# A zero-write on POOL between the additions of a depthwise convolution

## The chip, the core and the metric

The kernel runs on one core of one Trainium2 chip. The metric is the device time of one execution in microseconds. TensorE (PE) multiplies, VectorE (DVE), ScalarE (ACT) and GpSimd (POOL) do the elementwise work, SyncE (SP) and POOL issue DMAs.

## The reference

The computation is a two-layer decoder trunk over 512 tokens of width 1024, in float32. Layer 0 is a Conformer convolution module and a SwiGLU feed-forward; layer 1 is grouped-query attention in a sliding window over a shared K/V, and a second feed-forward. What matters here is the convolution module:

```python
a = glu(x @ w_pw1 + b_pw1)                      # first pointwise projection
y = causal_depthwise_conv(a, w_dw) + b_dw       # 31 taps, each channel by itself
y = silu(layernorm(y, ln_g, ln_b))
h = h + y @ w_pw2 + b_pw2                       # second pointwise projection
h = h + swiglu_ffn(rmsnorm(h), w_up, w_down)
```

## The kernel before

Channels lie on the partitions in eight tiles of 128; the 512 tokens are worked in two halves of 256 columns. The depthwise convolution of one half (class `Half`) goes through the channel tiles in pairs. Of the 31 taps of a tile some go to DVE, which multiplies and adds in one instruction into a PSUM bank (L1009). The others go to ACT and POOL: ACT makes the product of a tap in one of eight buffers `pr` (L1001), POOL adds it to the running sum (L1002). In the second half 17, 15, 15 and 15 taps of a tile go this way, for the four pairs. At the end of a tile POOL adds the two sums (L1013), ACT squares the result (L1038), and TensorE sums over the channels with a matrix of ones (L1052, L1058).

The first half's convolution runs beside the first projection. The second half's runs on, as a background job, beside the first half's second projection (`pw2`, L378, then L1143 for the residual) and the first part of its feed-forward (`ffn_part`, `ffn_up`); `pace` advances it by due points, one call per weight chunk. Before that job starts, 20 of its steps are taken beside the last first projections (`N_EARLY`) and 7 between the rows of the first half. A step of a pair advances both of its tiles by one DVE tap and by the products and additions that belong to it.

From the feed-forward on each weight chunk of 128x1024 is split into a rounded part `whi` (ACT, L294) and a remainder `wlo` (DVE, L297), and each product is three matmuls (L380 to L382): 24 for a chunk. The splits run up to three chunks ahead in four buffers. The norm before the feed-forward is taken late: TensorE sums the squares (L503), DVE finishes the mean (L505), POOL raises it to the power -1/2 (L507), ACT puts it on a diagonal (L515), TensorE spreads it over the partitions (L529), and the evacuation of the first pair of banks uses it.

The second half's feed-forward part 0 (`twin=True`) scales its result with the same spread norm on POOL (L606), and DVE adds it to the residual (L607).

Beside its arithmetic POOL issues DMAs that add weight blocks in DRAM (`prepare`, L289). Each is ordered behind the last instruction that went through the helper `pool_op`, which only notes that instruction. The helper `tc.issue_after(ins)` puts an instruction behind another on the same engine without a semaphore. The order of each engine's queue is otherwise made at compile time, from a schedule.

Of the kernel before, what the change touches and what calls it, by code (L numbers as in the profile page):

```python
# [11 lines left out]
F32 = mybir.dt.float32  # L12
# [6 lines left out]
P = 128  # L19
# [190 lines left out]
def hybrid_trunk(ctx: ExitStack, tc: tile.TileContext, xT, W, prm_in, wdw_in, sinks, relb, onehot, fin, lead, out):  # L210
    nc = tc.nc
    cpool = ctx.enter_context(tc.tile_pool(name="const", bufs=1))
# [9 lines left out]
    def uid(s):  # L222
        ctr[0] += 1
        return f"{s}{ctr[0]}"

    def bank():
        return ps.tile([P, 512], F32, tag="bank", name=uid("bank"))
# [4 lines left out]
    def temp():  # L232
        return tmp.tile([P, 512], F32, tag="tmp", name=uid("tmp"))
# [23 lines left out]
    def load(upto):  # L257
        while stream["dma"] < min(len(PLAN), upto):
# [3 lines left out]
            raws[i] = r  # L262
            stream["dma"] += 1

    def pool_op(op):
        pooled[0] = op.ins
        return op

    def copy_sums(name, lo, hi):
# [57 lines left out]
    def job(gen, *points):  # L327

        jobs.append([gen, points, 0])
# [32 lines left out]
    def get(*key):  # L362
        advance()
        pace()
        due[0] += rate[0]
        tick(int(due[0]))
        due[0] -= int(due[0])
        i = stream["use"]
        assert PLAN[i] == key, (PLAN[i], key)
        stream["use"] += 1  # L370
        hi, lo = splits.pop(i)
        n = {"kv": 4, "up": 4, "q": 4}.get(key[0], 2)
        sh = dict(a=n)
        return tuple(w and w.rearrange("p (a b) -> p a b", **sh) for w in (hi, lo))
# [32 lines left out]
    def mm2(out, w, x, start, stop):  # L407

        first, second = (w[0], x, out), (w[1], x[:, 0, :], out[:, 0, :])
        if stop:  # L410
            first, second = second, first
        nc.tensor.matmul(first[2], first[0], first[1], start=start, stop=False)  # L412
        nc.tensor.matmul(second[2], second[0], second[1], start=False, stop=stop)  # L413
# [59 lines left out]
    def col(name, i):  # L473
        c = PARAM_COLS[name] + i
        return prm[:, c:c + 1]
# [75 lines left out]
    def accs(w):  # L551
        if w == 512:
            return [bank() for _ in range(4)]
        return [b[:, e * w:(e + 1) * w] for b in (bank(), bank()) for e in range(2)]
# [8 lines left out]
    def down_group(keys, act_of, banks, on_step=None, on_m=None):  # L563
        nk = len(keys)
        w = banks[0].shape[-1]
        for ci, (key, kts) in enumerate(keys):
            whi, wlo = get(*key)
            order = [(k, m) for k in range(2) for m in range(4)]
            if ci == nk - 1:
                order = [(k, m) for m in range(4) for k in range(2)]  # L570
            for k, m in order:
                sl = slice(m * P, (m + 1) * P)
                mm3(banks[m], (whi[:, k, sl], wlo and wlo[:, k, sl]), act_of(kts + k),
                    ci == 0 and k == 0 and opens(m, w), ci == nk - 1 and k == 1 and closes(m, w))
                if on_step is not None and ci < nk - 1 and m == 3:
                    on_step()
                if on_m is not None and ci == nk - 1 and k == 1:
                    on_m(m)
                    if m % 2:
                        on_step()  # L580
            if on_step is not None and on_m is None and ci == nk - 1:
                on_step()
                on_step()

    def ffn_part(layer, part, xg, tok, rms, on_h=None, twin=False, plain=None):
        lo, hi = HALVES0[part]
        hid = ffn_up(layer, lo, hi, xg, tok, rms, twin, plain)
        w = tok.stop - tok.start
        for g in range(2):
            if twin:  # L590
                banks = [bank().rearrange("p (a s) -> p a s", a=2) for _ in range(4)]
                for kp in range(lo, hi):
                    whi, wlo = get("down", layer, kp, g)
                    order = [(k, m) for k in range(2) for m in range(4)]
                    if kp == hi - 1:
                        order = [(k, m) for m in range(4) for k in range(2)]
                    for k, m in order:
                        sl = slice(m * P, (m + 1) * P)
                        mm2(banks[m], (whi[:, k, sl], wlo[:, k, sl]), hid.both(2 * (kp - lo) + k),
                            kp == lo and k == 0, kp == hi - 1 and k == 1)  # L600
                rs_bc = rms.step2()
                for m, b in enumerate(banks):
                    t, hm = temp()[:, 0:w], h[g * 4 + m][:, tok]
                    nc.scalar.copy(t, b[:, 1, :])
                    nc.vector.tensor_add(t, b[:, 0, :], t)
                    pool_op(nc.gpsimd.tensor_mul(t, t, rs_bc))  # L606
                    nc.vector.tensor_add(hm, hm, t)  # L607
                continue
            if w == 256:

                full = [bank().rearrange("p (a s) -> p a s", a=2) for _ in range(2)]
                banks = [b[:, e, :] for b in full for e in range(2)]
            else:
                banks = accs(w)
            down_group([(("down", layer, kp, g), 2 * (kp - lo)) for kp in range(lo, hi)],
                       lambda kt: hid[kt], banks)
            if w == 256:
                rs_bc = rms.step2().unsqueeze(1).to_broadcast([P, 2, w])
                for e, b in enumerate(full):
                    i = g * 4 + 2 * e  # L620
                    nc.vector.tensor_mul(b, b, rs_bc)
                    nc.vector.tensor_add(hT[:, i:i + 2, tok], b, hT[:, i:i + 2, tok])
                    for k in range(2 if on_h is not None else 0):
                        on_h(i + k)
                continue
            for m in range(4):
                t = h[g * 4 + m][:, tok]
                nc.vector.tensor_add(t, banks[m], t)
                if on_h is not None:
                    on_h(g * 4 + m)  # L630
# [303 lines left out]
    with tc.tile_pool(name="conv", bufs=2) as cv:  # L934
# [41 lines left out]
        class Half:  # L976
# [7 lines left out]
            def taps(self, ct, c):  # L984
                n_pool = N_POOL[self.hf][ct // 2]
                a = a_pad[ct][:, self.hf * W2:(self.hf + 1) * W2 + PAD]
                yt = self.y[:, ct, :]

                def tap(j):
                    return wdw[:, ct, j:j + 1]  # L990

                nd = TAPS - n_pool
                acc, pi = None, 0
                for i in range(nd):
                    while pi * nd < n_pool * (i + 1):
                        j = nd + pi
                        pr = cv.tile([P, W2], F32, tag="pr", name=uid("pr"), bufs=8)
                        if acc is None:
                            on_act = nc.scalar.activation(pr, a[:, j:j + W2], AF.Identity, scale=tap(j), bias=col("bdw", ct))
                        else:  # L1000
                            on_act = nc.scalar.mul(pr, a[:, j:j + W2], tap(j))  # L1001
                            on_pool = pool_op(nc.gpsimd.tensor_add(pr, acc, pr))  # L1002
                        acc = pr
                        pi += 1
                    src = a[:, i:i + W2]
                    if i == 0 and ct < 4:
                        nc.vector.tensor_scalar(c, src, tap(i), None, op0=ALU.mult)
                    else:
                        on_dve = nc.vector.scalar_tensor_tensor(yt if i == nd - 1 else c, src, tap(i),  # L1009
                                                                c if i else self.shift, op0=ALU.mult, op1=ALU.add)  # L1010
                    yield
                self.last = on_act.ins, on_dve.ins, on_pool.ins
                pool_op(nc.gpsimd.tensor_add(yt, yt, acc))  # L1013
# [186 lines left out]
        for at_, (hf, ct) in enumerate(projs):  # L1200
# [13 lines left out]
            while done < n_taps * min(1, (at_ + 1) / 11):  # L1214
                next(taps, None)
                done += 1
# [23 lines left out]
            late.gate()  # L1240
        h1.after = [h0.silu]
        base = seen[0]
        job(second, (base, 0), (base + 8, 19), (base + 13, 22), (base + 26, 40), (base + 30, 45), (base + 34, 50), (base + 35, h1.n_steps - early - 3))
        x0 = {"ffn0": Pairs(KT)}
        plain = quads.tile([P, KT, W2], F32, tag="quad", name=uid("plain"))
# [70 lines left out]
    job(rows0.sums(), (base + 11, 0), (base + 19, 8), (base + 26, 14), (base + 32, 17))  # L1316
    pw2(h1.z, n1)
    ffn_part(0, 0, x0["ffn0"], HALF[1], n1.rms, twin=True)
    flush()

# [30 lines left out]
    if True:  # L1351
# [24 lines left out]
        for half in range(2):  # L1376
# [7 lines left out]
            if half == 0:  # L1384
                rs_bc = rms.step2()
# [312 lines left out]
```

## Time and profile before

| | us |
|---|---|
| median of 3 runs (1043.19 to 1044.5) | 1043.42 |
| the profiled execution | 1043.27 |
| its span, first to last instruction | 1041.5 |
| TensorE busy in the span | 1031.5 |
| POOL busy in the span | 473.2 |
| POOL's additions L1002, 208 of them | 155.4 |

A line of a timeline reads: start in microseconds from the start of the span, length, engine, line of the kernel, operation, tiles written and read, shapes, count of merged instructions, and in brackets the idle time of the engine before it with what ended that. A line of a group has busy time, mean duration in ns of one, and idle time before. A line of waits has the waiting instruction, what it waited for, the total in microseconds, how often, and the longest.

### The profile page before, as it was taken

How to read it: one execution, taken by the hardware profiler on the slowest of the kernel's cores; microseconds unless marked ns; L12 is line 12 of the kernel's file. 1: busy time of each engine (PE TensorE's matmuls, PEld its weight loads, DVE VectorE, ACT ScalarE, POOL GpSimd, SP SyncE). 2: the span in 40 equal slices, each digit the busy share in tenths (PEclk: the TensorE clock that was granted, in tenths of full speed). 3: DMA queues.
4: the chain of work that ended last, by engine and by line, in shares of the span. 5: the costliest groups of instructions: out<-in, count | busy, mean ns of one | idle time of the engine just before them, and what ended most of it. 6: DMA issues, size and time to landing. Idle time of an engine off the chain costs nothing.

```text
span 1041.5 us, 17709 instructions
## 1 busy us (share of the span) xinstructions
PE 1031.5 (99%) x6580; PEld 932.6 (90%) x6580; DVE 776.5 (75%) x1202; ACT 613.0 (59%) x1062; POOL 473.2 (45%) x569
## 2 busy tenths in 40 slices
PE   9999999999999999999999999999999999999996
PEld 8888889999988999998888877788989999898995
DVE  3999989978789777673536566678686877868777
ACT  3887798847776556552333565466655556554654
POOL 3999999930535233221214255405442334434134
PEclk9999999999999999999999999999999999999998
DMA  9999747999999988999969766955879988877742
GB/s 356 340 315 207 205 126 204 272 256 275 249 239 262 304 220 284 256 301 244 286 209 254 210 183 183 228 154 152 252 230 312 287 264 264 245 233 222 224 150 81
DMA packets 67282, 248.33 MB, mean 238 GB/s; under 512 B 7579, under 2 KB 13884, under 8 KB 66364
## 3 DMA queue, kind: packets, MB, share of 16 engines
q1 hardware_dynamic: 54236, 200.75, 55.9%
q0 software_dynamic: 12672, 46.14, 24.8%
q8 instruction: 51, 0.84, 0.3%
q10 hardware_dynamic: 288, 0.31, 0.1%
q14 instruction: 35, 0.29, 0.1%
HBM read 241.93 MB, written 97.52 MB: 326 GB/s over the span
## 4 chain that ended last, share of the span: by engine, by line
PE 98%; DMA 0%; DVE 0%; issue 0%; POOLq 0%; SPq 0%; POOL 0%; ACT 0%
PE bank L380 20%; PE bank L382 20%; PE bank L381 20%; PE bank L960 10%; PE bank L902 9%; PE bank L412 4%; PE bank L378 4%; PE bank L413 2%; PE bank L1441 1%; PE bank L1483 1%; PE bank L1470 1%; PE bank L1058 1%; PE bank L1607 1%; PE bank L948 1%; DMA both<-in_lead_dram 0%; PE bank L1562 0%
## 5 line engine op out<-in xcount | busy, mean ns | idle before, releaser
L297 DVE TENSOR_TENSOR wlo<-raw,whi 128x1024 fp32r<-128x1024 f32 x246 | 329.7, 1348 | 136.8 <-ACT whi L294 136.5
L294 ACT CAST whi<-raw 128x1024 fp32r<-128x1024 f32 x246 | 257.1, 1049 | 276.6 <-PE bank L381 194.1
L380 PE MATMUL bank<-quad,whi 128*128 128x256 f32 (+1 forms) x976 | 307.4, 317 | 0.0
L381 PE MATMUL bank<-quad,whi 128*128 128x256 f32 (+1 forms) x976 | 306.6, 315 | 0.0
L382 PE MATMUL bank<-quad,wlo 128*128 128x256 f32 (+1 forms) x976 | 305.7, 315 | 0.0
L380 PEld LDWEIGHTS bank<-quad,whi 128*128 128x128 f32 x976 | 185.5, 191 | 12.8 <-issue 1.6
L381 PEld LDWEIGHTS bank<-quad,whi 128*128 128x128 f32 x976 | 186.0, 191 | 11.9 <-issue 0.5
L382 PEld LDWEIGHTS bank<-quad,wlo 128*128 128x128 f32 x976 | 185.6, 191 | 11.8 <-issue 0.4
L853 POOL TENSOR_TENSOR up<-up 128x512 f32<-128x512 f32 x34 | 62.9, 1851 | 283.6 <-ACT up L850 283.6
L1002 POOL TENSOR_TENSOR pr<-pr,pr 128x256 f32<-128x256 f32 x208 | 155.4, 788 | 2.6 <-ACT pr L1001 2.5
L380 PE MATMUL bank<-rows,whi 128*128 128x256 f32 x488 | 138.0, 283 | 0.0
L381 PE MATMUL bank<-rows,whi 128*128 128x256 f32 x488 | 137.8, 282 | 0.0
L382 PE MATMUL bank<-rows,wlo 128*128 128x256 f32 x488 | 137.8, 282 | 0.0
L1009 DVE SCALAR_TENSOR_TENSOR bank<-apad,wdw,bank 128x256 f32<-128x256 f32 x248 | 112.4, 485 | 3.4
L1001 ACT ACTIVATE pr<-apad,wdw 128x256 f32<-128x256 f32 x208 | 98.3, 502 | 14.9 <-POOL pr L1002 13.1
L960 PE MATMUL bank<-quad,w 128*128 128x256 f32 x448 | 98.7, 380 | 0.0
L960 PEld LDWEIGHTS bank<-quad,w 128*128 128x128 f32 x448 | 84.9, 190 | 11.8 <-DVE bank L1009 0.2
L380 PEld LDWEIGHTS bank<-rows,whi 128*128 128x128 f32 x488 | 93.1, 191 | 0.3
L381 PEld LDWEIGHTS bank<-rows,whi 128*128 128x128 f32 x488 | 93.1, 191 | 0.3
L382 PEld LDWEIGHTS bank<-rows,wlo 128*128 128x128 f32 x488 | 93.0, 191 | 0.0
L491 POOL TENSOR_TENSOR tmp<-tmp,tmp 128x256 f32<-128x256 f32 (+1 forms) x28 | 26.8, 957 | 101.4 <-ACT tmp L487 96.2
L412 PE MATMUL bank<-quad,whi 128*128 128x512 f32 x168 | 59.7, 398 | 0.0
(230 smaller groups left out, 1635.9 us busy)
## 6 DMA issues: line engine op xcount, KB each, us to landing
raw<-in_W_dram SPq DMA_DIRECT2D x170, 512.0 KB, 5.7
raw<-sum SPq DMA_DIRECT2D x88, 512.0 KB, 5.4
sum<-in_W_dram SPq DMA_DIRECT2D x52, 512.0 KB, 6.2
sum<-in_W_dram POOLq DMA_DIRECT2D x44, 512.0 KB, 9.6
sum<-sum POOLq DMA_DIRECT2D x44, 512.0 KB, 8.5
sum<-in_W_dram SPq DMA_DIRECT2D x4, 3584.0 KB, 30.4
w<-in_W_dram SPq DMA_DIRECT2D x14, 512.0 KB, 8.6
sum<-in_W_dram SPq DMA_DIRECT2D x4, 1024.0 KB, 30.3
```

Of the source, the lines that this page charges most:

```text
L294: on_act = nc.scalar.copy(hi, src).ins
L297: latest[:] = [on_act, lo_engine[0].tensor_sub(lo, src, f32(hi)).ins]
L380: nc.tensor.matmul(out, w[0], x[0], start=start, stop=False, **kw)
L381: nc.tensor.matmul(out, w[0], x[1], start=False, stop=False, **kw)
L382: nc.tensor.matmul(out, w[1], x[0], start=False, stop=stop, **kw)
L412: nc.tensor.matmul(first[2], first[0], first[1], start=start, stop=False)
L853: pool_op(nc.gpsimd.tensor_mul(gate, gate, c[:, m, :, 1, :]))
L902: nc.tensor.matmul(out, x, w[:, ws], start=first and e == 0 and i == 0, stop=e == 1 and i == 2, skip_group_check=True)
L960: mm = nc.tensor.matmul(self.pb[:, w * W2:(w + 1) * W2], w1_of(ct, w, k), x[k] if x else xg[k][:, tok], start=k == 0, stop=k == KT - 1)
L1001: on_act = nc.scalar.mul(pr, a[:, j:j + W2], tap(j))
L1002: on_pool = pool_op(nc.gpsimd.tensor_add(pr, acc, pr))
L1009: on_dve = nc.vector.scalar_tensor_tensor(yt if i == nd - 1 else c, src, tap(i), c if i else self.shift, op0=ALU.mult, op1=ALU.add)
```

## The change

A tile `letting` of 128x64 zeros-to-be is allocated where the second projection's stage begins, after the early steps. From there on a new helper, `let_go`, follows each convolution addition of POOL and each POOL product of the twin part with a memset of that tile. Nothing reads the tile. The memset goes through `pool_op`, so the next sum DMA of POOL is ordered behind it.

```diff
+    letting = []
+
     def pool_op(op):
         pooled[0] = op.ins
+        return op
+
+    def let_go(op):
+        if letting:
+            with tc.issue_after(op.ins):
+                pool_op(nc.gpsimd.memset(letting[0], 0.0))
         return op
...
-                    pool_op(nc.gpsimd.tensor_mul(t, t, rs_bc))
+                    let_go(pool_op(nc.gpsimd.tensor_mul(t, t, rs_bc)))
                     nc.vector.tensor_add(hm, hm, t)
...
-                            on_pool = pool_op(nc.gpsimd.tensor_add(pr, acc, pr))
+                            on_pool = let_go(pool_op(nc.gpsimd.tensor_add(pr, acc, pr)))
...
         base = seen[0]
+        letting.append(cpool.tile([P, 64], F32, tag="letting", name="letting"))
         job(second, (base, 0), (base + 8, 19), (base + 13, 22), (base + 26, 40), (base + 30, 45), (base + 34, 50), (base + 35, h1.n_steps - early - 3))
```

## The prediction

> **What bounds the kernel now.** I read the page's busy times and its chain first, then TensorE's waits, then the 20 us windows of the stage that the change touches, then each engine's timeline there.
>
> ```profile
> span 1041.5 us, 17709 instructions
> PE   1031.5 (99%) x6580; PEld 932.6 (90%) x6580; DVE 776.5 (75%) x1202; ACT 613.0 (59%) x1062; POOL 473.2 (45%) x569
> PE 98%; DMA 0%; DVE 0%; issue 0%; POOLq 0%; SPq 0%; POOL 0%; ACT 0%
> ...
> PE bank L465 <- POOL ones_m L462: 1.1, 1, 1.1
> PE bank L948 <- DVE quad L922: 0.7, 2, 0.4
> ```
>
> TensorE is 98% of the chain that ended last, and its list of waits has two entries, both in the first microseconds (a warm-up and the first input). From the second projection to the end nothing makes it wait. Its pace does not depend on POOL either:
>
> ```profile
> 180.00:200.00 20.00, 20.00 (x168) 19.95 (x167) 18.91 (x24) 18.54 (x34) 18.16 (x21) 1.00 1.01 290
> 240.00:260.00 20.00, 20.00 (x169) 20.00 (x168) 16.16 (x31) 14.96 (x28) 0.00 (x0) 1.00 0.90 277
> ```
>
> The columns are PE, PEld, DVE, ACT, POOL, granted clock, DMA share, GB/s. With POOL busy for 18.16 us TensorE issues 168 matmuls in 20 us, with POOL idle 169, at clock 1.00 both times. So an edit on POOL can shorten nothing that sets the end; it can lengthen the run, if it makes something late that TensorE's queue contains. The question is which result of POOL has the smallest lead over TensorE.
>
> **What the change adds.** One memset of 128x64 behind each convolution addition (L1002) that is built after the zero tile exists. By the code the second half has then taken 20 early steps and 7 more: its first pair of channel tiles (15 steps) and 12 of the 16 working steps of its second pair, 11 of 14 additions in each of the two tiles. Left are 6 + 28 + 28 = 62 additions. The twin part's L606 adds 8 more. Nothing is removed. The memset becomes what the next sum DMA of the POOL queue is issued behind.
>
> The price of one. The trace has no 64-wide memset, but narrower and wider ones in a row, and the additions beside which it will stand:
>
> ```profile
> 0.94 0.20 POOL masks.py:197 MEMSET ident<- 128x128 f32 x1
> 1.08 0.20 POOL L469 MEMSET mean_m<- 128x128 f32 x1
> ...
> 1.40 0.12 POOL L937 MEMSET apad<- 128x30 f32 x1
> ...
> 1.81 0.47 POOL L937 MEMSET apad<- 128x30 f32 x7
> ...
> 7.38 4.87 POOL L491 TENSOR_TENSOR tmp<-tmp,tmp 128x256 f32<-128x256 f32 x6 [1.59 <-ACT tmp L487]
> ...
> 53.03 7.60 POOL L1002 TENSOR_TENSOR pr<-pr,pr 128x256 f32<-128x256 f32 x11
> ```
>
> A 128-wide memset starts 0.14 us after the one before it; seven 30-wide ones fit in 0.47 us, 0.067 each. In between, 64 columns: 0.067 + 34/98 x 0.073 = 0.09 us, my value. The other end: additions in a row take 0.69 us each (7.60 over 11), yet where each needs the one before it 0.81 (4.87 over 6). If the memset also breaks that overlap it costs 0.09 + 0.12 = 0.21 us. The lower end is 0, where POOL waits anyway; below nothing is excluded, since the additions keep their work.
>
> The Trainium skill, Perfetto Trace Analysis, section GPSIMD Engine Instruction, says that spans of this engine are not to be trusted and that start-to-start spacing is to be used; the trace agrees (the 128-wide memset shows 0.20 and the next starts after 0.14). By the shown spans, 0.12 for 30 columns and 0.20 for 128, a 64-wide one would be 0.15, and the sum below would come out at the late root's price, slower.
>
> Where they fall. The tightest result of POOL is the norm's reciprocal root (L507) in the first feed-forward part: ScalarE makes a diagonal of it (L515), and TensorE has the matmul that spreads it (L529) at a fixed place in its queue.
>
> ```profile
> L1002 POOL TENSOR_TENSOR pr<-pr,pr 128x256 f32<-128x256 f32 x36 | 29.2, 844 | 0.7 <-ACT pr L1001 0.6
> ...
> 148.76 1.91 POOL L1002 TENSOR_TENSOR pr<-pr,pr 128x256 f32<-128x256 f32 x2 [0.62 <-ACT pr L1001]
> ...
> 151.51 3.34 POOL L1002 TENSOR_TENSOR pr<-pr,pr 128x256 f32<-128x256 f32 x4
> ...
> 155.49 7.11 POOL L1002 TENSOR_TENSOR pr<-pr,pr 128x256 f32<-128x256 f32 x10
> 162.56 7.81 POOL L1002 TENSOR_TENSOR pr<-pr,pr 128x256 f32<-128x256 f32 x8
> ...
> 178.61 0.71 POOL L507 TENSOR_TENSOR rs<-ms,mhalf 128x2 f32<-128x2 f32 x1
> ...
> 176.76 0.15 DVE L505 TENSOR_SCALAR ms<-bank 128x2 f32<-128x2 f32 x1
> ...
> 179.35 0.69 ACT L515 ACTIVATE tmp<-ident,rs 128x128 f32<-128x128 f32 x2 [2.19 <-POOL rs L507]
> ...
> 181.43 0.59 PE L529 MATMUL bank<-tmp,ones_m 128*128 128x256 f32 x2
> ```
>
> The first line is POOL's groups from 139.6 to 178.6 us, the others timelines. L507's input is there at 176.91; it starts at 178.61, when POOL comes to it. L515 ends at 180.04 and TensorE arrives at 181.43: a lead of 1.39 us. Of the 62 additions 36 lie before L507. I go through them:
> - The first 10 (139.6 to 148): 0.9 us, of which POOL's idle 0.7 (its wait for ScalarE's products) takes most; 0.2 is left.
> - 6 from 148.76 to 154.8 and 8 from 162.56: nothing. There DVE and POOL alternate. The 8 take 0.98 us each instead of 0.69 (7.81 over 8), so each addition waits 0.3 us for DVE, and a memset of 0.09 fits into that. The rows of DVE that show it:
>
> ```profile
> 164.47 0.95 DVE L537 SCALAR_TENSOR_TENSOR quad<-h,prm,quad 128x256 fp32r<-128x256 f32 x1
> ...
> 160.84 0.48 DVE L537 SCALAR_TENSOR_TENSOR quad<-h,prm,quad 128x256 fp32r<-128x256 f32 x1
> ...
> 176.83 1.22 DVE L297 TENSOR_TENSOR wlo<-raw,whi 128x1024 fp32r<-128x1024 f32 x1
> ...
> 187.24 3.45 DVE L297 TENSOR_TENSOR wlo<-raw,whi 128x1024 fp32r<-128x1024 f32 x1
> ...
> 186.51 3.08 POOL L1002 TENSOR_TENSOR pr<-pr,pr 128x256 f32<-128x256 f32 x4
> ```
>
> - 10 from 155.49, at POOL's own pace (0.71 us each): 10 x 0.09 = 0.9. The last 2 before L507: 0.18.
>
> Sum: 0.2 + 0.9 + 0.18 = 1.3 us later at L507, against a lead of 1.39. TensorE does not wait: 0 us. If no memset hides, 36 x 0.09 - 0.7 = 2.5 us, and TensorE waits 1.15 us, still little.
>
> After L507 come 26 additions, 26 x 0.09 = 2.3 us, 5.5 at 0.21. Their cover:
>
> ```profile
> 206.84 1.86 POOL L1002 TENSOR_TENSOR pr<-pr,pr 128x256 f32<-128x256 f32 x2
> 216.54 2.42 POOL L1013 TENSOR_TENSOR y<-y,pr 128x256 f32<-128x256 f32 x2 [7.84 <-DVE y L1009]
> ...
> L607 DVE TENSOR_TENSOR h<-h,tmp 128x256 f32<-128x256 f32 x7 | 4.5, 665 | 0.2 <-POOL tmp L606 0.2
> ```
>
> POOL is done with them at 208.70 and then waits 7.84 us for DVE's taps. That covers either end. Without the cover the late sum would reach TensorE's L1058 directly. The 8 memsets behind L606 stand behind products for which DVE (L607) waited 0.2 us in all: 8 x 0.09 = 0.7 us, not on the path. The sum DMAs of POOL's queue start by the same fraction of a microsecond later.
>
> What DVE gains. Four additions in a row keep its weight split waiting at 187.24: 3.45 us instead of 1.22. A memset between them, which reads nothing, gives DVE a gap: up to 2.2 us there. TensorE does not wait for that split, so it is worth nothing at the end. The Trainium skill, SBUF — State Buffer, section Who interferes with whom, says that a DVE instruction with two SBUF inputs contends with a POOL instruction that reads SBUF and not with one that only writes; the trace agrees as far as the 3.45 goes, and no row here shows the memset's side.
>
> Forecast: the profiled execution took 1043.27 us, 1.8 more than its span; the median of the runs is 1043.42. With 0 added: **1043.4 us**. A measurement of this kernel tells 0.2%, 2.1 us, from no change.
>
> **The rivals.**
>
> Slower, the late root. Place: L529 at 181.43. Price: at 0.15 per memset, the middle between 0.09 and 0.21, with none hidden, 36 x 0.15 - 0.7 - 1.39 = 3.3 us, 1046.7; at 0.21, 5.5 us, 1048.9. It decides from 36 m - 0.7 - 1.39 = 2.1 on, m = 0.116 us with none hidden, 0.19 with the 14 hidden ones left out. For it: 0.116 is not far above my value, and the lead is nearly used up already. Against it: the alternation rows. Chance 0.22.
>
> Slower, another order. The order of each engine's queue comes from a schedule made at compile time, and 70 more instructions on POOL can move others. TensorE has no wait to lose, so this can only cost. The smallest lead of a weight split:
>
> ```profile
> 172.17 0.47 PE L380 MATMUL bank<-quad,whi 128*128 128x256 f32 x1
> ...
> 196.13 1.61 DVE L297 TENSOR_TENSOR wlo<-raw,whi 128x1024 fp32r<-128x1024 f32 x1
> ...
> 199.13 0.28 PE L380 MATMUL bank<-quad,whi 128*128 128x256 f32 x1
> ```
>
> Counted in chunks of 24 matmuls from 172.17, the tenth opens at 199.13 and uses this split, done at 197.74, in its third matmul: 1.6 us. Put behind one more blocked split of 3.45 it costs 1.8 us, behind two 5.3; the middle is 3.6, 1047.0. For it: the interleaving of POOL's queue does not follow the source. Against it: TensorE's order in this stage does, chunk by chunk. Chance 0.15.
>
> Faster, the freed port. Were TensorE paced by DVE after all, 3.45 - 1.22 = 2.2 us would come back: 1041.2. Against it stands the empty list of waits. Chance 0.06.
>
> Not what it says: the memsets end up together where POOL is idle, and nothing moves: 1043.4. Chance 0.04.
>
> **How the numbers follow.** The forecast has 0.53, and it takes in waits below 2.1 us. With the last rival, within 0.2%: 0.57; slower 0.22 + 0.15 = 0.37; faster 0.06. For 8 in 10 the range leaves out the faster case (0.06) and the dearest part of the slower ones (some 0.14): from 1042.4 to 1048.0.
>
> **What would show it.** In the changed profile: 70 memsets of 128x64, starting some 0.09 us before what follows; L507 about 1.3 us later; no wait of TensorE at L529; splits of DVE between 182 and 207 us nearer to 1.22 us; POOL's wait before L1013 shorter. A wait of TensorE at L529 of 2 us or more, or a new one on a weight split, would make the prediction wrong, and so would a TensorE stream that is shorter with POOL's gaps in it.

## Result, and the profile after

| | before | changed |
|---|---|---|
| median of 5 runs | 1043.42 us | 1052.17 us (1051.58 to 1052.81) |
| ratio to before | | 1.0083, 95% interval 1.0069 to 1.0096 |
| span of the profiled execution | 1041.5 us | 1051.0 us |

The changed kernel is slower by 8.75 us. Its lines stand 8 higher than those of the kernel before: L297 is the sum DMA, L305 the low half of a weight split, L390 the matmul that uses it, L515, L523 and L537 the root, its diagonal and the matmul that spreads it, L1010 the convolution addition, L1021 the last addition of a block. The memset is L274.

First the page of the changed kernel (busy times and chain), then its list of TensorE's waits:

```profile
PE 1034.2 (98%) x6580; PEld 934.3 (89%) x6580; DVE 785.5 (75%) x1202; ACT 612.6 (58%) x1062; POOL 477.4 (45%) x639
PE 90%; DVE 3%; ACT 2%; POOL 2%; issue 2%; DMA 1%; POOLq 0%; SPq 0%; DVEq 0%; ACTq 0%
```

```profile
PE bank L390 <- DVE wlo L305: 4.4, 1, 4.4
PE bank L537 <- ACT tmp L523: 1.9, 1, 1.9
PE bank L956 <- DVE quad L930: 1.2, 2, 0.9
```

The instructions are those of before and 70 memsets (POOL 569, now 639). POOL's share of the span has not moved, TensorE's chain share has fallen from 98% to 90%. Two waits are new, and both are single ones; the third row stands in the first microseconds, as before. The timeline of TensorE shows where they are, and one row of the kernel before shows the matmul that now waits longest; the windows of the changed kernel (PE, PEld, DVE, ACT, POOL, granted clock, DMA share, GB/s) show what follows each wait:

```profile
184.23 0.48 PE L537 MATMUL bank<-tmp,ones_m 128*128 128x256 f32 x1 [1.94 <-ACT tmp L523]
206.85 0.38 PE L390 MATMUL bank<-quad,wlo 128*128 128x256 f32 x1 [4.41 <-DVE wlo L305]
```

```profile
199.37 0.28 PE L382 MATMUL bank<-quad,wlo 128*128 128x256 f32 x1
```

```profile
184.20:187.60 3.40, 3.37 (x26) 3.32 (x27) 2.38 (x4) 3.40 (x7) 3.40 (x8) 1.00 1.02 265
206.80:210.20 3.40, 3.35 (x17) 3.35 (x18) 3.40 (x7) 2.62 (x5) 0.65 (x1) 0.56 0.65 164
```

TensorE's queue has the same order in both kernels, so the start of each matmul can be compared with its own start before:

- 0.7 us of the 9.5 us between the spans lies ahead of the first real matmul (the first input came later in this execution); it is not the change. 9.5 - 0.7 = 8.8 us, as between the medians. POOL runs 0.6 us later as well before it meets its first memset: the addition ahead of that one began at 138.85 before and begins at 139.48 now.
- At L537 the delay grows by 2.1 us (181.43 to 184.23, less the 0.7).
- At L390 by 4.7 us more (199.37 to 206.85 is 7.5 us; 2.8 were there already).
- Behind that wait the clock is 0.56 on average over 3.4 us: 17 matmuls instead of 28 at their spacing of 0.12 us. By the end of it the delay has grown by 1.6 us (the matmul of 203.09 before starts at 212.16, 9.1 us later). Behind the wait of 1.94 us the clock stays at 1.00.
- The rest to the end is 0.5 us, with no wait over 0.4 us.

Behind both waits stands POOL. Here are its timeline ahead of the root and the splits of DVE:

```profile
164.18 0.82 POOL L1010 TENSOR_TENSOR pr<-pr,pr 128x256 f32<-128x256 f32 x1
...
174.21 2.32 POOL L1021 TENSOR_TENSOR y<-y,pr 128x256 f32<-128x256 f32 x2
176.47 1.02 POOL L297 DMA_DIRECT2D sum<-in_W_dram  x1
...
179.50 1.03 POOL L1052 TENSOR_TENSOR sq<-sq,sq 128x256 f32<-128x256 f32 x1
180.18 1.69 POOL L274 MEMSET letting<- 128x64 f32 x7
181.81 0.81 POOL L297 DMA_DIRECT2D sum<-in_W_dram  x1
182.35 0.43 POOL L274 MEMSET letting<- 128x64 f32 x1
182.46 0.99 POOL L515 TENSOR_TENSOR rs<-ms,mhalf 128x2 f32<-128x2 f32 x1
```

```profile
177.96 3.66 DVE L305 TENSOR_TENSOR wlo<-raw,whi 128x1024 fp32r<-128x1024 f32 x1 [0.68 <-ACT whi L302]
...
187.78 4.80 DVE L305 TENSOR_TENSOR wlo<-raw,whi 128x1024 fp32r<-128x1024 f32 x1
...
201.18 5.63 DVE L305 TENSOR_TENSOR wlo<-raw,whi 128x1024 fp32r<-128x1024 f32 x1
...
212.75 4.51 DVE L305 TENSOR_TENSOR wlo<-raw,whi 128x1024 fp32r<-128x1024 f32 x1
```

The root starts at 182.46 instead of 178.61, 3.85 us later, 0.6 of it the later start of this execution. The block's last additions are 3.15 us late (before, from 171.06), and seven memsets in one lot (1.69 us) stand between the sum of squares and the root. And four splits take 3.66 to 5.63 us instead of 1.21; before there was one, of 3.45. The split of 201.18 is the one for which L390 waits. What POOL does in that time:

```profile
200.21 0.35 POOL L274 MEMSET letting<- 128x64 f32 x2
200.50 0.81 POOL L297 DMA_DIRECT2D sum<-in_W_dram  x1
201.07 1.01 POOL L1010 TENSOR_TENSOR pr<-pr,pr 128x256 f32<-128x256 f32 x1
201.75 0.41 POOL L274 MEMSET letting<- 128x64 f32 x1
201.86 0.98 POOL L1010 TENSOR_TENSOR pr<-pr,pr 128x256 f32<-128x256 f32 x1
202.53 0.40 POOL L274 MEMSET letting<- 128x64 f32 x1
202.64 1.64 POOL L1010 TENSOR_TENSOR pr<-pr,pr 128x256 f32<-128x256 f32 x2
203.98 0.39 POOL L274 MEMSET letting<- 128x64 f32 x1
204.08 1.62 POOL L1010 TENSOR_TENSOR pr<-pr,pr 128x256 f32<-128x256 f32 x2
205.43 0.37 POOL L274 MEMSET letting<- 128x64 f32 x1
```

A sum DMA is issued, six additions and four memsets follow without a gap, and the split gets to work when they are through (201.18 + 5.63 - 1.21 = 205.6). Additions and memsets begin some 0.3 us before the one ahead has ended (201.07 + 1.01 = 202.08, and the memset behind starts at 201.75). In this stage, in every run, that much is seen only behind an issue; up to 0.15 us builds up in some executions over a long row of additions without one (here by 148 us). In the kernel before, too, the split of 3.45 us stands behind an issue, at 185.88. And far outside this stage it has a longer one, unchanged in all runs of the whole kernel: 8.07 us at 705.96, behind the issue of 705.00 and three POOL products of 128x1024 in a row; TensorE does not wait for it.

All long splits of this stage, in every run below, have a POOL DMA issue ahead of POOL's run. The reverse does not hold. Behind the issue of 201.36 in the kernel before, a split got in ahead of the first addition, which had to wait for it (1.32 us), and from there on POOL and DVE took turns.

### The profile page after: what moved, and what is told of

Read it like the earlier page. It is cut to its first block, busy times and chain, and to the rows that moved or that the text cites. A ratio compares the mean times of both kernels' runs of the same rounds, so it can differ in the third digit from the quotient of the medians.

```text
span 1051.0 us, 17750 instructions
## 1 busy us (share of the span) xinstructions
PE 1034.2 (98%) x6580; PEld 934.3 (89%) x6580; DVE 785.5 (75%) x1202; ACT 612.6 (58%) x1062; POOL 477.4 (45%) x639
## 4 chain that ended last, share of the span: by engine, by line
PE 90%; DVE 3%; ACT 2%; POOL 2%; issue 2%; DMA 1%; POOLq 0%; SPq 0%; DVEq 0%; ACTq 0%
PE bank L388 19%; PE bank L390 19%; PE bank L389 19%; PE bank L910 9%; PE bank L968 8%; PE bank L420 4%; PE bank L421 2%; PE bank L1450 1%; PE bank L1492 1%; DVE bank L1017 1%; PE bank L1479 1%; POOL pr L1010 1%; ACT pr L1009 1%; PE bank L1066 1%; PE bank L1616 1%
## 5 line engine op out<-in xcount | busy, mean ns | idle before, releaser
L305 DVE TENSOR_TENSOR wlo<-raw,whi 128x1024 fp32r<-128x1024 f32 x246 | 339.5, 1388 | 137.1 <-ACT whi L302 136.9
L390 PE MATMUL bank<-quad,wlo 128*128 128x256 f32 (+1 forms) x976 | 306.5, 315 | 4.4 <-DVE wlo L305 4.4
L390 PEld LDWEIGHTS bank<-quad,wlo 128*128 128x128 f32 x976 | 186.3, 191 | 16.4 <-DVE wlo L305 4.6
L1010 POOL TENSOR_TENSOR pr<-pr,pr 128x256 f32<-128x256 f32 x208 | 156.1, 847 | 6.5 <-ACT pr L1009 6.5
L390 PE MATMUL bank<-rows,wlo 128*128 128x256 f32 x488 | 137.8, 282 | 0.0
L390 PEld LDWEIGHTS bank<-rows,wlo 128*128 128x128 f32 x488 | 93.0, 191 | 0.0
```

The lines of the kernel that those rows point to most:

```text
L305: latest[:] = [on_act, lo_engine[0].tensor_sub(lo, src, f32(hi)).ins]
L390: nc.tensor.matmul(out, w[1], x[0], start=False, stop=stop, **kw)
L1010: on_pool = let_go(pool_op(nc.gpsimd.tensor_add(pr, acc, pr)))
```

## Experiments

Three theories were set against each other. A: the root is late, and the rest follows from that. B: the memsets of the last pair of blocks make the port busier and DVE late. C, which came from the traces of the first runs: right behind a DMA issue POOL does not give up the port that it shares with DVE until it has nothing ready (the hold, below), and the memsets shift and lengthen such runs.

**Which memsets.** Three kernels with a part of them; the conv addition's edit, and in the third only the twin's memsets stay:

```
e1:  on_pool = pool_op(add);  if ct >= 6: let_go(on_pool)     # twin without memset
e2:  on_pool = pool_op(add);  if ct < 6:  let_go(on_pool)     # twin without memset
e3:  on_pool = pool_op(add)                                    # twin with memset
```

> Memsets only behind the 28 additions of the last pair of channel tiles; 26 of them lie behind the root L507, none of the 34 before it is left, and the twin part has none. Theory A (the root first): the late root is what makes POOL run behind, and the blocked weight splits only follow from it; without memsets before the root both waits of TensorE vanish, 1043.4 +- 1 us. Theory B (the port by itself): a memset between two additions does not give DVE the port, it only fills the gaps in which DVE got it; TensorE does not wait at L529, but a split near 200 us is blocked for 4 us or more and TensorE waits for it, 1045 to 1049 us.

> Memsets only behind the 34 additions of the second and third pair, all before the root L507; none later, none in the twin part. Theory A: both waits of TensorE stay, 2 us at L529 and 4 to 5 us for a split near 200 us, 1050 to 1052 us. Theory B: only the wait at L529 stays, 1045.5 us, and the splits near 200 us are as before, at most 3.5 us.

> Only the 8 memsets behind the products of the twin part, and the zero tile. Both theories: no wait of TensorE, 1043.4 +- 1 us. If the tile's place or the new schedule alone cost something, it shows here.

Measured beside a median of 1044.88 for the kernel before: e1 1043.83 us, ratio 0.9989 (0.9979 to 0.9999); e2 1047.68, 1.0038 (1.0024 to 1.0052); e3 1045.08, 1.0003 (0.9993 to 1.0012). So 28 memsets in the last pair cost nothing where the root is on time: a split is blocked there as B had it (4.51 us at 206.86), but TensorE does not wait for it. The 34 others cost 2.8 us by the medians and 3.9 by the means, a third to a half of the loss and less than A had (1050 to 1052), more than B (1045.5); three of the nine runs of e2 took 1050.8 to 1051.9. Neither alone gives 8.75 us: the last pair's memsets cost their part only when POOL is late already. In e2 TensorE waits 1.6 us at L537 and 1.1 us in two waits at L390, behind splits of 4.53 and 2.85 us at 184.64 and 193.64, where there are no memsets any more. In e3, with none in the convolution, one split is long beside that of 187 us, which the kernel before has too:

```profile
194.61 0.80 POOL L297 DMA_DIRECT2D sum<-in_W_dram  x1
195.18 4.44 POOL L1010 TENSOR_TENSOR pr<-pr,pr 128x256 f32<-128x256 f32 x6
199.41 0.97 POOL L297 DMA_DIRECT2D sum<-in_W_dram  x1
```

```profile
196.37 4.35 DVE L305 TENSOR_TENSOR wlo<-raw,whi 128x1024 fp32r<-128x1024 f32 x1
```

Again an issue and a run, and the split gets in when the next issue comes. Memsets are not needed for it; where it falls decides what it costs (1.0 us of wait at L390 here, where no theory had a wait, and nothing for the 4.51 us in e1).

**The port by itself.** A bench of splits, additions and memsets, without DMA issues:

> Not the trunk: a kernel of twelve short stretches, which leaves out the whole computation. In each stretch POOL runs 12 additions of 128x256 and DVE beside it 4 splits of 128x1024 with two SBUF inputs; both are released by the same ACT copy. Stretches: splits alone (1.22 us each), additions alone (0.69 apart), both, then the additions with a memset of 128x64 behind each (alone and with the splits), memsets alone in one tile and in twelve, memsets beside splits, additions with a copy of 64 columns behind each, additions that each wait for a fresh product of ACT (two buffers, one buffer), and two memsets behind each addition. If a memset opens the port (what the prediction took from the trace and the Trainium skill): with memsets each split waits for one addition at most, 4 splits in about 4 x 1.9 = 7.6 us. If POOL keeps the port over the memset (Theory B): the first split waits until the last addition is done, 9 to 10 us, and then 1.2 us each; only additions that wait for a product let DVE in.

Rows of its POOL timeline: twelve additions alone; two additions with a memset between; twelve memsets of one tile; twelve of twelve tiles.

```profile
11.99 8.20 POOL L46 TENSOR_TENSOR sum<-src 128x256 f32<-128x256 f32 x12 [11.55 <-ACT src L40]
...
42.34 0.72 POOL L46 TENSOR_TENSOR sum<-src 128x256 f32<-128x256 f32 x1
43.00 0.15 POOL L49 MEMSET zero<- 128x64 f32 x1
43.10 0.72 POOL L46 TENSOR_TENSOR sum<-src 128x256 f32<-128x256 f32 x1
...
59.66 2.44 POOL L49 MEMSET zero<- 128x64 f32 x12
...
62.72 1.10 POOL L49 MEMSET zero<- 128x64 f32 x12
```

A memset between additions costs 0.76 - 0.68 = 0.08 us, in a lot on one tile 0.20, because each waits for the one before it, on different tiles 0.09. Beside splits an addition and a split take turns, 1.74 us each, with and without memsets, also when the addition waits for a product of ScalarE. Beside memsets alone a split takes 1.21 us, as it does by itself (1.22). Nothing here keeps a split waiting for more than one addition, so the bench did not have what the kernel has. What it lacked was the DMA issue.

> Leaves out the whole computation: ten stretches, each started by a copy of ACT, with DVE splits of 128x1024 and POOL additions of 128x256, as in the earlier bench, in which a POOL addition and a split took turns (1.74 us a split) with and without memsets. Here most stretches start with a DMA issue on POOL's queue. Theory C (behind a DMA issue POOL's additions run on without giving up the shared port until POOL has nothing ready): the splits of stretches 2, 3, 4, 6, 7 and 10 wait for the whole run of additions (12 x 0.69 = 8 us, 24 x 0.69 = 16 us in stretch 10), in stretch 8 only from the issue on, and those of stretch 5 (a chain without an issue) take turns; in stretch 4 the wait of a memset for the one before it on the same tile (57 ns) tells if a gap that short is enough to let DVE in. Theory D (it is the chain, each addition reading the sum before it): splits of 5, 6 and 7 wait for the whole run, those of 2, 3 and 8 take turns. Theory of turns: no split over 1.8 us anywhere.

That bench did not test it: its additions had to wait for ScalarE between the issue and the splits, and after such a wait they took turns (36 splits, 1.61 us on average). Only two stretches had additions right behind an issue. In the first, with no DVE beside them, the rows overlapped, 1.04 us at a pitch of 0.68. In the eighth the first addition had to wait for the last split, which was under way, and the rest showed 0.71 at 0.68, without the overlap. So it was built again, with the issue behind the second addition and DVE coming in with the end of the fourth:

> Leaves out the whole computation: eleven stretches, in each of which POOL begins with two additions of 128x256, in most of them goes on with a DMA issue, and then runs twelve more additions (24 in stretch 7), while DVE comes with four splits of 128x1024 once the fourth addition is done. In the bench before this one the additions behind an issue had to wait for ACT first, and every split took 1.74 us; there the additions of stretch 1, right behind an issue and with no DVE beside them, showed records of 1.04 us at a pitch of 0.68. Theory C in its present form (right behind a DMA issue, with no wait between, POOL's instructions overlap and the port is not given up until POOL stops or comes to another issue): in stretches 2, 3, 5, 6 and 8 the first split waits for the rest of the run, some 10 x 0.68 = 7 us, in stretch 7 some 22 x 0.68 = 15 us; one memset between (3, 6) does not let DVE in and lengthens the wait by 0.1 us each, a pair of one tile (4) may; stretches 1, 10 and 11 without an issue take turns, 1.74 us a split; 9 takes turns where an addition waits for its product. Theory of phase (no hold behind an issue, something else in the kernel keeps DVE waiting): 1.74 us throughout.

The first splits of stretches 1 (no issue), 2 (issue), 3 (issue, memset behind each addition), 4 (two memsets of one tile), 5 (a chain), 7 (24 additions), 10 (memsets, no issue):

```profile
9.10 1.66 DVE L43 TENSOR_TENSOR lo<-src,hi 128x1024 fp32r<-128x1024 f32 x1
...
24.77 7.72 DVE L43 TENSOR_TENSOR lo<-src,hi 128x1024 fp32r<-128x1024 f32 x1
...
41.13 8.58 DVE L43 TENSOR_TENSOR lo<-src,hi 128x1024 fp32r<-128x1024 f32 x1
...
59.17 1.22 DVE L43 TENSOR_TENSOR lo<-src,hi 128x1024 fp32r<-128x1024 f32 x1
...
76.86 1.78 DVE L43 TENSOR_TENSOR lo<-src,hi 128x1024 fp32r<-128x1024 f32 x1
...
109.68 15.80 DVE L43 TENSOR_TENSOR lo<-src,hi 128x1024 fp32r<-128x1024 f32 x1
...
167.74 1.75 DVE L43 TENSOR_TENSOR lo<-src,hi 128x1024 fp32r<-128x1024 f32 x1
```

This is theory C by itself. One issue ahead, and a split waits for all that POOL has ready: the rest of the twelve additions, or of the 24. A memset between them opens nothing, it makes the wait 0.86 us longer. A wait of 57 ns (the second memset of a pair) ends it, and so does a chain in which each addition waits for the one before (78 ns): there the theory's number, 7 us, was wrong, for stretch 5 and for 6, the chain with memsets (1.78 us in both). Stretch 9 missed too: with products made ahead the split took 7.73 us. Stretch 8, with copies of 64 columns, held as expected (9.45 us), and 11, a chain without an issue, took turns. In the kernel two tiles' chains alternate, so an addition does not wait for the one just ahead, and a run can hold.

One place in the changed kernel goes further. Behind the issue of 183.23 POOL's addition of 185.61 had to wait for a product of ScalarE (done at 185.53), and the split of 185.15 got in at once (1.28 us); yet the additions behind it still overlap, 1.28 us at a pitch of 0.70, and the next split, at 187.78, was held, 4.80 us. So a gap lets DVE in, but not every gap ends the state.

**The same in the kernel: the issues held back.**

```
 base = seen[0]
+withheld.append(True)      # sum DMAs wait for the end of the conv statistics
```

> The changed kernel with POOL's accumulating DMA issues (L297) held back until the conv statistics of the second half are done (they then come in one lot, some ten of them). Theory C: without issues between 175 and 230 us no split of that stretch takes over 2 us, TensorE's wait of 4.4 us at L390 is gone, and the time is 1043 to 1046 (the late root alone, up to 1.9 us at L537, less if the issues ahead of the root made it late), unless the lot of issues afterwards costs something of its own, which the kernel before with the same hold shows. Theory A (the late root alone does it, and all the rest follows from it): waits at L537 and L390 stay, 1050 to 1052.

> The kernel before with the same hold, the control of the run with held issues: splits of 187 us fall from 3.45 to 1.8 or less by theory C; the time is 1043.4 if the lot of issues afterwards is harmless, and whatever it is over that is the price of the lot and not of the memsets.

Measured beside 1043.59: e6, the changed kernel with its issues held back, 1054.40 us, 1.0107 (1.0092 to 1.0122); e7, the kernel before with the same, 1051.78, 1.0077 (1.0060 to 1.0094). TensorE's waits in e6, then in e7:

```profile
PE bank L511 <- POOL tmp L499: 4.1, 1, 4.1
PE bank L421 <- DVE wlo L305: 2.1, 2, 1.6
PE bank L537 <- ACT tmp L523: 1.3, 1, 1.3
```

```profile
PE bank L503 <- POOL tmp L491: 4.0, 1, 4.0
PE bank L413 <- DVE wlo L297: 1.2, 1, 1.2
```

The wait at L390 is gone, and no split between 175 and 235 us takes over 1.80 us in e6, or 1.83 in e7. The lot of issues afterwards makes the next norm late by itself (4.0 us at L503, from 275 us on), with or without memsets. What the memsets still cost is 1054.40 - 1051.78 = 2.6 us, against 8.75 with the issues in place; 1.3 us of them are the root's wait. The expected 1043 to 1046 was missed by the price of the lot, which only the control showed.

**The state broken, the issues left in place.** Behind each of the first twelve issues a pair of memsets of one more tile, the additions held behind them:

```
 op = nc.gpsimd.dma_start(summed[c], ..., accum_op=ALU.add, ...)
+if n < 12:
+    for _ in range(2):
+        with tc.issue_after(op.ins):
+            op = pool_op(nc.gpsimd.memset(pause[0], 0.0))
+    behind[0] = op.ins      # conv additions, y, yy, sq: issue_after(behind[0])
...
```

> The changed kernel with two more memsets, of one tile of their own, right behind each of the first twelve DMA issues of POOL's queue, and the additions held behind them. The second waits for the first; in the bench such a wait (57 ns) ended the state behind an issue in which POOL does not give up the port. The issues stay where they are, 0.5 us of memsets come on top of each, three of them ahead of the root. Theory C: no split between 175 and 230 us takes over 2.8 us, TensorE's wait of 4.4 us at L390 is gone or under 1 us, the root's wait stays or grows (1.9 to 3.4 us), and the time is 1045.5 to 1048 against 1052. Theory of lateness alone (the long splits follow from where POOL's bursts fall, not from the issues): waits at L390 stay, 1052 to 1054.

> The kernel before with the same pairs behind its issues, and no other memset: the control. By theory C its split of 3.45 us at 187 us falls to 1.8 or less; TensorE does not wait for that split, so the time stays at 1043.4, or rises by up to 1 us where two pairs ahead of the root use up its lead of 1.39 us.

Measured beside 1043.74: e11 1053.35 us, 1.0090 (1.0076 to 1.0104); e12 1047.69, 1.0036 (1.0024 to 1.0049). TensorE's new waits, e11 and then e12:

```profile
PE bank L1073 <- POOL yy L1064: 3.7, 1, 3.7
PE bank L547 <- ACT tmp L533: 2.7, 1, 2.7
```

```profile
PE bank L1065 <- POOL yy L1056: 2.7, 1, 2.7
```

The mechanism came as expected: no split from 175 to 235 us over 1.80 us in either, and no wait on a split. The time did not; in e11 it even falls on the numbers of lateness alone, 1052 to 1054, though not one of its long splits is there. The pairs make POOL's own results late: the root in e11 (2.7 us) and, in both, the sums of the conv statistics (L1073, L1065), which the prediction had taken as covered. So the hold may be not only a loss: while DVE waits, POOL gets its sums done. With the hold broken in this way the memsets still cost 1053.35 - 1047.69 = 5.7 us, more than with the issues held back, so how much of the 8.75 us the hold is worth depends on how it is taken away. Whether the pairs' own time or the order imposed behind them makes those sums late was not told apart.

**The lot in front of the root.** Eight tiles in turn for the memsets, so that none waits for the one before it; and the kernel before with a lot of 38 memsets ahead of the root and no others:

```
e8:   letting.extend(tile ... for i in range(8));  letting.append(letting.pop(0)) behind each memset
e10:  if ct == 5:  38 memsets behind on_pool, tiles in turn, each issue_after(pooled[0])
```

> The changed kernel with eight tiles in turn for the memsets, so that a memset does not wait for the one before it. In piles a memset then takes 0.09 us as in the bench, not 0.21. Some 12 memsets ahead of the root stand in piles: 12 x 0.11 = 1.3 us earlier, and by theory A TensorE's wait at L537 falls from 1.9 to 0.6 us and the time to about 1048 or less. By theory C the runs of additions behind DMA issues still hold the port, the waits at L390 of 2 to 5 us stay, and the time stays at 1047 to 1051.

> The kernel before with one lot of 38 memsets of 128x64 (eight tiles in turn, 0.09 us each, 3.3 us in all) behind the last addition of the sixth block, ahead of the root, and no other. It makes POOL's stream late at one place and lengthens no run behind an issue. If lateness ahead of the root is the cause of the root's wait and also shifts the later runs of additions against the splits: TensorE waits 1.3 to 2.3 us at L529, some split between 184 and 205 us takes over 2.8 us, and the time is about that of the run with memsets before the root alone, 1046 to 1049. If memsets between the additions are needed for the long splits: the wait at L529 alone, no split over 3.5 us, 1045 to 1046.

e8: 1050.35 us, 1.0066 (1.0051 to 1.0081). The lots are gone, a memset stands behind every addition, and the root is as late as ever (182.55); its wait is 2.3 us, and the matmul on `wlo` (L391 in this kernel) waits 1.9 us. Theory A's number for it, 0.6 us, fell: the lot of seven was not an extra on top of the memsets' sum. e10: 1043.39, 0.9994 (0.9984 to 1.0004); it says nothing on lateness, because the schedule put the lot in groups of three to eight between POOL's other work, only 24 of the 38 ahead of the root, and the root came only 0.2 us later (178.84; 0.5 with the 0.3 us by which this execution began earlier). It does show that 24 memsets can stand ahead of the root and cost TensorE nothing.

## Why the prediction was wrong, by its own steps

- **The bound: right.** TensorE had nothing to gain. All but 0.5 us of the loss is waits of TensorE in one stage, and the slow clock behind one of them.
- **The price of a memset: right where it stands between additions** (0.09 us against 0.08). Alone in lots of one tile it is 0.20, near the upper end, which the prediction had given for another reason.
- **The root's delay, 1.3 us: mis-sized; 3.2 us**, which is 3.85 less the 0.6 that POOL was late at its first memset. By the prediction's own list the first 16 additions cost 0.6 (it had 0.2), the ten from 155.49 cost 0.3 (it had 0.9), the eight from 162.56 cost 1.5 (it had 0), and from the block's end to the root 0.7 (it had 0.18). The term that failed is "6 from 148.76 to 154.8 and 8 from 162.56: nothing. There DVE and POOL alternate". The last eight additions took 8.5 us to the block's end before (162.56 to 171.06), an issue of 0.75 among them, and take 10.0 (164.18 to 174.21), without one: memsets in threes of one tile (0.57 us, twice), and turns lost to splits that had met an issue or the block's end before. TensorE was 0.7 us later itself, so its lead of 1.39 us stands against the 3.2: 1.8 us; measured were 1.94. This is the rival of the late root, at its place but below its price: 3.2 us is 36 memsets at 0.11 us with the 0.7 us of idle off, just short of the 0.116 from which it was to decide. The range would have held it alone.
- **"A memset between them, which reads nothing, gives DVE a gap": wrong in sign.** The 3.45 us at 187.24 were put down to four additions in a row. What held the port was the DMA issue ahead of them, at 185.88, a row next to those that were read. The Trainium skill, SBUF — State Buffer, section Who interferes with whom, calls the port pair that the two engines share an exclusive lock, which goes by issue order, and says that a POOL instruction that only writes does not contend with a DVE instruction with two SBUF inputs. Without an issue the benches agree (1.66 us a split beside additions, 1.75 with memsets between them, 1.21 beside memsets alone); behind an issue a split took 7.72 us, waiting for some ten instructions, and a writing one between them did not let it in. There the measurement decides.
- **The cover behind L507, 7.84 us: it held for POOL's own sums and was the wrong thing to cover.** POOL still waited 10.5 us there for DVE's taps. The cost went another way, through the splits: 4.4 us at L390 and 1.6 us of slow clock behind it, which the forecast had at 0.
- **The rival of another order: right place, wrong cause.** The wait fell on the tenth chunk's split, and with two blocked splits ahead 5.3 us had been worked out; measured were 4.4. TensorE's order had not changed; POOL's runs had shifted against the issues and the splits.
- **The rivals were priced as alternatives.** They came together, and the first fed the second: with the root late DVE is late (185.15 for the split that began at 181.02), POOL's products gather, and a longer run meets each issue. e1 and e2 show it: alone the two parts cost nothing and 2.8 to 3.9 us, all 70 together 8.75. 3.3 + 3.6 us over 1043.4 would have been 1050.3, near the result and outside the range; that the two errors add up so near to it is in part luck, for the late root was priced too high and the blocked split too low.

How the memsets turned one long split into four is read from the traces: POOL came late to each issue, with more additions ready. That longer runs, and not the mere shift, did the last part was not tested by itself.

## What to carry to other kernels

Where POOL issues DMAs between elementwise work, look in the trace for DVE instructions with two inputs that take several times their normal time, and then for an issue at the head of POOL's run: in these runs a step right behind the issue that waits for POOL's own step before it ended the hold, but made POOL's own results later, so both leads have to be known. Where several engines' leads are near one or two microseconds, add the rivals that lie on one path instead of choosing among them. Give an experiment that moves work elsewhere its control on the kernel before: here the control carried 8 of the 11 us.

## What the runs showed of the hardware that was not expected

- Behind a DMA issue of POOL's queue, additions showed 1.00 us at a pitch of 0.68, and 0.72 without one; behind an issue a split of DVE took up to 15.80 us, without one it waited for at most one addition (1.78 us). A wait of 57 ns of a POOL instruction for the one before it ended this in the bench. The Trainium skill, Perfetto Trace Analysis, section DMA Instruction — SWDGE (GPSIMD), says that two of POOL's processors, 0 and 1, generate the descriptors. That these then lag behind the others, so that one addition starts on some before it ends on others and the port is never seen free, would fit the overlapping rows; no run here shows it.
- TensorE's clock fell to half for 3.4 us behind a wait of 4.41 us in the changed kernel, and the length of the wait alone does not decide it. Behind 2.28 us (e8, at the root) and 1.65 us (e6, at L421) it fell too, behind 1.94 us (changed, at the root) and 2.67 us (e12, at L1065) it did not. Windows of e8, e6 and e12, each just behind the wait:

```profile
184.00:187.40 3.40, 3.36 (x15) 3.25 (x16) 2.37 (x4) 3.40 (x7) 2.75 (x6) 0.56 1.04 273
333.50:336.90 3.40, 3.40 (x14) 2.92 (x13) 3.40 (x5) 2.49 (x4) 0.00 (x0) 0.50 1.05 251
207.60:211.00 3.40, 3.40 (x25) 3.30 (x26) 3.05 (x5) 0.29 (x1) 3.40 (x4) 1.00 0.95 316
```

  Where it fell it cost some 1.6 us on top of the wait (the changed kernel). The Trainium skill, TensorE: Matmul & The Clock Gate, section Part 1: The HAM clock gate, puts the fall behind an idle window of about 3.4 us; here less was enough twice, and twice it was not.
